# Two-layer diffusion trunk on one core: changes of stage in written order, with twelve modulation chunks

## Chip, cores and metric

One NeuronCore of a Trainium2 chip runs the whole kernel. The metric is the device time of one execution in microseconds; the median of three runs stands for a kernel. TensorE (PE) does matmuls and transposes, ScalarE (ACT) and VectorE (DVE) evict, split and scale, GpSimd (POOL) does only small powers, SyncE (SP) issues nearly all DMA transfers.

## The reference

Two streams of 128 tokens, context (stream 0) and latent (stream 1), go through two layers. Each layer is an attention stage and an MLP stage; each of these normalises the stream, scales and shifts it by a modulation that comes from a conditioning vector, and adds its gated, normalised result to the stream.

```python
for l in range(DEPTH):                       # DEPTH = 2
    m = silu(cvec) @ w_ada[l] + b_ada[l]     # 6 x 2048: shift, scale, gate of both stages
    h = rms_norm(x, g0) * (1 + scale) + shift
    o = mix(h @ w_in[l])                     # neighbourhood, grouped-query, differential heads
    x = x + gate * rms_norm(o @ w_out[l], g1)
    h = rms_norm(x, g2) * (1 + scale') + shift'
    u = square(relu(h @ w_up[l])) @ w_down[l]
    x = x + gate' * rms_norm(u, g3)
```

All is in fp32 accuracy. The weights are some 600 MB, which each execution reads once.

## The kernel before

**Trunk matmuls.** A weight chunk is 1 MB: 128 partitions by 2048 numbers. `split_to` (L1012) cuts each half of it into a high part `wh` (ACT, L1020) and a low part `wl` (DVE, L1021), both rounded to the fast matmul type; three pairs of buffers hold them (`NW = 3`). The activations `XT` (four tiles, one per 512 columns, both streams) are split the same way, and `Group.run` (L350) makes three matmuls per product (L365 to L367) for two streams and two column tiles. A group of eight chunks fills four accumulators in PSUM; the last chunk of a group is run whole, accumulator by accumulator, and each is evicted by `done` when it is full.

**Modulation.** `w_ada` takes two ways. A chunk on PE (`ada_mm`, L139) adds eight narrow matmuls to one PSUM tile; after eight chunks (a set of two blocks) ACT copies it to `pt` (L151), PE transposes that, DVE sums it and makes scale, shift or gate. A chunk on DVE (`dv_mul`, L206) costs two passes over 2048 columns, one per stream, against the rows `sB`. `DV_BLOCKS` and `PE_BLOCKS` at the head of the file say which block goes where.

**Loads.** `items` is the list of chunks in order. `issue` (L1003) asks for the next chunk whenever fewer than `NRAW = 5` raw buffers are in use; all go through SP's queue. Where a PE modulation chunk has been multiplied, or both halves of a weight chunk have been split, its buffer is free. `ahead` (L722) loads four modulation chunks into the XT buffers, which are idle by then.

**A change of stage.** The accumulators of the last group are evicted in the order (tile 2, stream 0), (3, 0), (2, 1), (3, 1). `residual` (L316) sums the squares, raises them to -1/2 on POOL, adds to the stream `x` in four pieces (L326), squares each (ACT, L330) and computes the next norm. `after_attn` (L886) and `after_mlp` (L975) run the chunks left over: four from raw buffers (`TAIL = 4`) and the four held ones. Then `make_xt` (L261) scales a block of 512 columns (DVE for stream 0, L269; ACT for stream 1, L271), transposes it on PE and applies scale and shift (L280, L282), high half (L287) and low half (L288). There are three such changes: layer 0 attention to MLP, layer 0 MLP to layer 1 attention, layer 1 attention to MLP.

**What sets the order.** The program is a list of tiles and operations. A planner orders each engine's instructions: it takes, by a model of times, the first one in written order whose inputs it believes ready; so work written later can get in front. `behind` (L109) forbids this for two pairs: the `wl` splits stay behind the last add of stream 0, and one square of stream 1 stays behind a `pt` copy. `load_sb`, `reload_sb` and `store_x` (L195, L202, L306) are DMA issues that are written behind the handover and are free to be issued earlier.

## Time and profile before

| | us |
|---|---|
| median of 3 runs | 2296.63 (2293.83 to 2298.72) |
| the profiled execution | 2295.36 |
| its span, first to last instruction | 2293.3 |
| PE busy | 2223.2 |
| DVE busy | 1592.6 |
| ACT busy | 1072.2 |

The page of a profile gives busy times, groups of instructions and waits of one execution; the queries on the trace give the same for a stretch. In a timeline a row is: start and length in us, engine, source line, operation, out<-in with shapes, how many instructions were merged, and in brackets the idle time of the engine before it and what ended that. A busy PE may run at half clock, so the granted clock (PEclk, 1.00 is full) has to be read beside it.

### The profile page before, as it was taken

The numbers are of one execution on the slowest core, as the hardware profiler recorded it, in microseconds if no ns is written. First come the engines' busy times: TensorE is split into PE (matmuls) and PEld (weight loads), VectorE is DVE, ScalarE is ACT, GpSimd is POOL, SyncE is SP. The second block draws the span as 40 slices with busy tenths as digits, with TensorE's granted clock in tenths as the row PEclk, the third lists the DMA queues.
The fourth block names the chain that finished last, engine by engine and source line by source line (L and its number), as shares of the span: only waits on it lengthen the run. The fifth ranks groups of instructions, "written<-read, shape, count | busy, mean of one in ns | idle before, by whom it ended". The sixth has DMA issues, their size and how long they took to land.

```text
span 2293.3 us, 26818 instructions
## 1 busy us (share of the span) xinstructions
PE 2223.2 (97%) x10460; PEld 1746.8 (76%) x10460; DVE 1592.6 (69%) x1967; ACT 1072.2 (47%) x1483; POOL 23.3 (1%) x30
## 2 busy tenths in 40 slices
PE   6999999999999999999999999999999999999997
PEld 3667666678888888888867777876888888888886
DVE  2566745499899998999668787548566566565445
ACT  4334444365445434434446455545544543443443
POOL 0000000000000000000000000000000000000000
PEclk9999999999999999999999999999999999999999
DMA  8888787978788887788868666766566566556652
GB/s 335 313 336 333 300 313 309 397 295 298 295 310 300 298 302 294 282 295 313 317 225 299 237 248 218 270 232 230 205 230 233 203 220 236 205 211 223 221 189 93
DMA packets 94539, 611.40 MB, mean 267 GB/s; under 512 B 14026, under 2 KB 16458, under 8 KB 22730
## 3 DMA queue, kind: packets, MB, share of 16 engines
q1 hardware_dynamic: 93836, 609.21, 72.1%
q8 instruction: 82, 1.34, 0.2%
q10 hardware_dynamic: 576, 0.48, 0.1%
q14 instruction: 45, 0.37, 0.0%
HBM read 601.97 MB, written 7.68 MB: 266 GB/s over the span
## 4 chain that ended last, share of the span: by engine, by line
PE 82%; DVE 7%; DMA 4%; ACT 3%; issue 2%; POOL 1%; SPq 0%; POOLq 0%; DVEq 0%; ACTq 0%
PE acc L366 25%; PE acc L367 25%; PE acc L365 25%; DVE wl L1021 3%; PE m L120 3%; PE ada L147 2%; DMA raw<-w_adaT_in 2%; ACT wh L1020 1%; ACT qT L918 1%; DMA raw<-w_in_in 1%; POOL st L107 1%; DMA raw<-w_ada_in 1%; DVE junk L212 1%; PE m L456 1%; DVE stg L326 0%
## 5 line engine op out<-in xcount | busy, mean ns | idle before, releaser
L1020 ACT ACTIVATE wh<-raw 128x1024 fp32r<-128x1024 f32 x720 | 759.2, 1060 | 961.1 <-PE acc L367 862.2
L1021 DVE TENSOR_TENSOR wl<-raw,wh 128x1024 fp32r<-128x1024 f32 x720 | 873.4, 1222 | 471.5 <-ACT wh L1020 469.7
L365 PE MATMUL acc<-wh,XT 128*128 128x512 f32 x1600 | 629.0, 399 | 10.8 <-ACT XT L287 5.9
L366 PE MATMUL acc<-wl,XT 128*128 128x512 f32 x1600 | 629.5, 394 | 4.9 <-DVE wl L1021 4.6
L367 PE MATMUL acc<-wh,XT 128*128 128x512 f32 x1600 | 625.9, 392 | 0.0
L366 PE MATMUL acc<-wl,big 128*128 128x512 f32 x1280 | 500.8, 391 | 1.3 <-DVE wl L1021 1.1
L365 PE MATMUL acc<-wh,big 128*128 128x512 f32 x1280 | 498.3, 393 | 0.6 <-ACT wh L1020 0.3
L367 PE MATMUL acc<-wh,big 128*128 128x512 f32 x1280 | 498.1, 390 | 0.0
L365 PEld LDWEIGHTS acc<-wh,XT 128*128 128x128 f32 x1600 | 301.3, 189 | 91.1 <-ACT wh L1020 14.1
L366 PEld LDWEIGHTS acc<-wl,XT 128*128 128x128 f32 x1600 | 301.9, 189 | 74.0 <-DVE wl L1021 13.4
L367 PEld LDWEIGHTS acc<-wh,XT 128*128 128x128 f32 x1600 | 301.7, 189 | 61.9
L365 PEld LDWEIGHTS acc<-wh,big 128*128 128x128 f32 x1280 | 239.9, 188 | 59.7 <-issue 5.0
L366 PEld LDWEIGHTS acc<-wl,big 128*128 128x128 f32 x1280 | 240.4, 188 | 53.3 <-DVE wl L1021 4.5
L367 PEld LDWEIGHTS acc<-wh,big 128*128 128x128 f32 x1280 | 240.4, 188 | 49.7
L212 DVE SCALAR_TENSOR_TENSOR junk<-raw,sB 128x2048 fp8e5<-128x2048 f32 x92 | 210.4, 2286 | 13.5 <-DMA raw<-w_adaT_in 13.0
L212 DVE SCALAR_TENSOR_TENSOR raw<-raw,sB 128x2048 f32<-128x2048 f32 x92 | 210.1, 2284 | 0.1
L147 PE MATMUL ada<-raw,sT 128*32 128x512 f32 (+1 forms) x768 | 95.0, 574 | 15.2 <-DMA raw<-w_ada_in 15.1
L147 PEld LDWEIGHTS ada<-raw,sT 128*32 128x32 f32 x768 | 20.8, 110 | 60.1 <-issue 36.6
L911 DVE TENSOR_TENSOR big<-tmp,big 128x512 fp32r<-128x512 f32 x64 | 43.8, 687 | 30.1 <-ACT big L910 29.8
L775 DVE TENSOR_TENSOR stg<-stg,acc 128x512 f32<-128x512 f32 x64 | 42.8, 684 | 27.6 <-PE acc L367 27.4
L918 ACT ACTIVATE qT<-acc 128x512 f32<-128x512 f32 x64 | 37.9, 594 | 18.9 <-PE acc L367 17.9
L107 POOL TENSOR_TENSOR st<-st,hf 128x1 f32<-128x1 f32 (+2 forms) x26 | 23.1, 894 | 2263.7 <-DVE st L106 2068.9
(123 smaller groups left out, 919.2 us busy)
## 6 DMA issues: line engine op xcount, KB each, us to landing
raw<-w_up_in SPq DMA_DIRECT2D x128, 1024.0 KB, 5.3
raw<-w_down_in SPq DMA_DIRECT2D x128, 1024.0 KB, 4.9
raw<-w_adaT_in SPq DMA_DIRECT2D x92, 1024.0 KB, 4.9
raw<-w_ada_in SPq DMA_DIRECT2D x80, 1024.0 KB, 7.3
raw<-w_in_in SPq DMA_DIRECT2D x72, 1024.0 KB, 6.4
raw<-w_out_in SPq DMA_DIRECT2D x32, 1024.0 KB, 6.2
XT<-w_ada_in SPq DMA_DIRECT2D x12, 1024.0 KB, 7.8
raw<-w_ada_in SPq DMA_DIRECT2D x16, 512.0 KB, 5.0
```

Source lines behind the costliest of these rows:

```text
L107: pool.tensor_tensor(out, out, hf[:, 0:width], ALU.pow)
L120: pe.transpose(out, in_, ident)
L147: pe.matmul(pa[32 * g:32 * g + 32, 0:w], sT[:, 4 * kq + g, 2 - 2 * t:34 - 2 * t], raw[:, g * w:(g + 1) * w], start=((t, kq) == (0, 0)), st ...
L212: p = dve.scalar_tensor_tensor(o, raw, 1.0, sB[v], ALU.mult, ALU.mult, accum_out=a[:, j, v:v + 1], saturate=None if v else False)
L365: pe.matmul(a, xh, wh[:, c], start=first, stop=False)
L366: pe.matmul(a, xh, wl[:, c], start=False, stop=False)
L367: pe.matmul(a, xl, wh[:, c], start=False, stop=last)
L775: dve.tensor_tensor(o, o, a, ALU.add)
L911: dve.tensor_tensor(A[:, :, 1, s * P:(s + 1) * P], uv, hi.bitcast(F32), ALU.subtract)
L918: act.activation(t, a, AF.Relu)
L1020: act.activation(wh, r, AF.Copy)
L1021: behind(dve.tensor_tensor(wl, r, wh.bitcast(F32), ALU.subtract), mark["res"])
```

## The change

Each change of stage becomes one item, `edge`, with its instructions on PE, ACT, DVE and POOL in the order in which the program is written. From the last chunk of a stage on, every instruction of these four engines is pinned behind the one written before it on its engine (`keep`, `Engine`), until `edge_run` ends; DMA issues on SP are not pinned. `behind` is used there no more.

- Twelve modulation chunks stand at each change: four held in XT buffers, eight from raw buffers (`TAIL = 8`), with the first weight chunk of the new stage loaded behind the fourth. In both attention stages the additional ones come out of the same stage's filling; in the layer 0 MLP one more block of layer 1 (`M_M[3]`, four chunks) goes from DVE to PE. A set that begins at the change has a PSUM tile of its own; the copies to `pt` (`ada_end`) come after the first weight chunk's matmuls.
- `residual` is cut into `res_scale`, `res_add` and `res_norm`; `edge_done` puts these between the evictions and writes a product with the gates after the scale it would delay.
- The first weight chunk is not split ahead: its two halves, and the high part of the third half chunk (the second weight chunk's first half), are split at written places (`split_part`).
- `make_xt` is cut into `xt_turn` (scale, transpose) and `xt_fin` (modulate, split). Block 0 is made in halves, stream 1's first half is turned before stream 0's second half is finished, and the first chunk's matmuls stand between. Block 1 follows; blocks 2 and 3 are made around the next chunks.
- At the end of the kernel the last residual uses the same pieces in the written order.

The core of the diff:

```diff
 NACC = 4
-TAIL = 4
...
-DV_BLOCKS = [G_M, M_A + M_M[:4] + G_A[:3] + G_M]
-PE_BLOCKS = [M_A[2:] + G_A + M_M, M_M[4:] + G_A[3:]]
+DV_BLOCKS = [G_M, M_A + M_M[:3] + G_A[:3] + G_M]
+PE_BLOCKS = [M_A[2:] + G_A + M_M, M_M[3:] + G_A[3:]]
...
+        def __getattr__(self, name):
+            f = getattr(self.e, name)
+            def g(*a, **k):
+                i = f(*a, **k)
+                if mark["keep"]:
+                    tc.keep_in_program_order(i)
+                return i
+            return g
+    pe, act, dve, pool = Engine(nc.tensor), Engine(nc.scalar), Engine(nc.vector), Engine(nc.gpsimd)
+    def keep(on):
+        mark["keep"] = on
...
-        end = t == len(blks) - 1 and kq == 3
+        key = (l, half, *blks)
+        if key not in ada_live:
+            two = mark["keep"] and len(blks) == 2
+            ada_live[key] = [psm() if two else ps.tile([P, 512], F32, tag="ada", bufs=1, name="ada"), 0]
+        pa, no = ada_live[key]
+        ada_live[key][1] += 1
+        end = no == 4 * len(blks) - 1
         for g in range(4):
...
         if end:
+            ada_over.append((l, blks, ada_live.pop(key)[0], 0 if half is None else 2 * half, w))
...
+    ada_over = []
+    def ada_end():
+        while ada_over:
+            l, blks, pa, j0, w = ada_over.pop(0)
             pt = sb([P, 512], "pt")
-            mark["pt"] = act.activation(pt[:, 0:w], pa[:, 0:w], AF.Copy)
-            fast.append(ada_post(l, blks, pt, 0 if half is None else 2 * half, w // P))
+            act.activation(pt[:, 0:w], pa[:, 0:w], AF.Copy)
+            fast.append(ada_post(l, blks, pt, j0, w // P))
 
...
+    def res_scale(ss, s):
         r = st2()
         dve.tensor_reduce(r[:, 0:1], ss[:, s, :], AX.X, ALU.add)
         rstd(r[:, 0:1], r[:, 0:1], D, 1)
+        return r
...
+    def res_add(rows, r, s, last):
         ss2 = st2()
...
+            dve.scalar_tensor_tensor(x[s][:, c], rows[s][:, c], r[:, 0:1], x[s][:, c], ALU.mult, ALU.add)
             if last:
...
+                act.activation(rows[s][:, c], x[s][:, c], AF.Square, accum_out=ss2[:, n:n + 1])
+        return ss2
+    def res_norm(s, ss2):
+        xr[s] = st2()
+        dve.tensor_reduce(xr[s][:, s:s + 1], ss2[:, 0:4], AX.X, ALU.add)
+        rstd(xr[s][:, s:s + 1], xr[s][:, s:s + 1], D, 1)
...
+    def edge_done(rows, ss, s, n, last, mul):
+        if (n, s) == (2, 0):
+            edge["mul"] = mul
+        elif (n, s) == (3, 0):
+            edge["mul"]()
+            edge["r0"] = res_scale(ss, 0)
+            mul()
+        elif (n, s) == (2, 1):
+            edge["ss2"] = res_add(rows, edge["r0"], 0, last)
+            edge["mul"] = mul
+        elif (n, s) == (3, 1):
+            edge["mul"]()
+            if not last:
+                nt[0] = sb([P, 4, 512], "big", 5)
+                res_norm(0, edge["ss2"])
+            edge["r1"] = res_scale(ss, 1)
+            mul()
+            edge["rows"] = rows
+        else:
+            mul()
+    def edge_run(l, w, held, g, ada, part, weights):
+        held(0, 1)
+        for i in range(4):
+            ada(i)
+        held(1, 3)
+        ada(4)
+        new_xt([0])
+        m = xt_turn(0, 0, 0, 2)
+        ada(5)
+        part(0, True, True)
+        part(1, True, False)
+        xt_fin(l, w, 0, 0, m, 0, 2)
+        g.open()
+        g.piece(0, 0, weights(0))
+        m = xt_turn(0, 0, 2, 4)
+        ss2 = res_add(edge["rows"], edge["r1"], 1, False)
+        part(1, False, True)
+        part(2, True, False)
+        res_norm(1, ss2)
+        held(3, 4)
+        ada(6)
+        m1 = xt_turn(0, 1, 0, 2)
+        xt_fin(l, w, 0, 0, m, 2, 4)
+        g.piece(0, 1, weights(1))
+        xt_fin(l, w, 0, 1, m1, 0, 2)
+        part(2, False, True)
+        ada(7)
+        m1 = xt_turn(0, 1, 2, 4)
+        g.piece(1, 0, weights(0))
+        xt_fin(l, w, 0, 1, m1, 2, 4)
+        new_xt([1, 2, 3])
+        m = xt_turn(1, 0, 0, 4)
+        g.piece(1, 1, weights(1))
+        g.cnt += 2
+        xt_fin(l, w, 1, 0, m, 0, 4)
+        ada_end()
+        keep(False)
+        xt_fin(l, w, 1, 1, xt_turn(1, 1, 0, 4), 0, 4)
+    def edge_items(l, w, tail, held, first):
+        items.append(("edge", tail[:4] + [first] + tail[4:], (l, w, held)))
...
+                mul = lambda: dve.tensor_tensor(S["rows"][s][:, c], S["rows"][s][:, c], a, ALU.mult)
+                edge_done(S["rows"], ssA[0], s, nt, False, mul)
...
-                if (nt, s) == (3, 0):
-                    residual(S["rows"], ssA[0], False, 0)
...
+            go = Group(2, KT, o_lhs(), wout_done(nh))
+            go.final = nh == 1
+            rest += tchunks(I["w_out"][l], 8 * nh, 8, go, ko, need)
...
-        weave(rest[cut:], fill[nf:], tail=TAIL)
...
-        def after_attn(S=S, l=l, use=use):
-            mark["tail"] = mark["pt"]
-            use()
-            drain_dv()
-            drain_fast()
-            new_xt()
-            mark["pt"] = mark["tail"]
-            residual(S["rows"], ssA[0], False, 1)
-        call(after_attn)
...
-            last = ada_items(1, G_A[3:] + M_M[4:5])
-            load, use = ahead(last[4:])
+            last = ada_items(1, M_M[4:5] + M_M[3:4] + G_A[3:])
+            load, use = ahead(last[8:])
...
+        first = rest.pop(0)
+        edge_items(l, 1, *end_attn, first)
+        rest.insert(0, ("call", lambda l=l: (drain_fast(), make_xt(l, 1, 2))))
+        rest.insert(2, ("call", lambda l=l: (drain_fast(), make_xt(l, 1, 3))))
...
-            g, m = dv_items(0, G_M), dv_items(1, M_A + M_M[:4])
+            g, m = dv_items(0, G_M), dv_items(1, M_A + M_M[:3])
...
-        def after_mlp(M=M, l=l, use=use):
-            if l + 1 < L:
-                mark["tail"] = mark["pt"]
-                use()
-                mark["pt"] = mark["tail"]
-            drain_fast()
-            residual(M["rows"], ssA[1], l == L - 1, 1)
...
+    def split_part(k, hi, lo):
+        i, j = subs[k]
+        if i not in raws:
+            return False
+        r = raws[i][:, j * 1024:(j + 1) * 1024]
+        if hi:
             wh = wp.tile([P, 1024], F32R, tag="wh", bufs=NW, name="wh")
             wl = wp.tile([P, 1024], F32R, tag="wl", bufs=NW, name="wl")
             act.activation(wh, r, AF.Copy)
-            behind(dve.tensor_tensor(wl, r, wh.bitcast(F32), ALU.subtract), mark["res"])
             splits[(i, j)] = (wh, wl)
+        if lo:
+            wh, wl = splits[(i, j)]
+            dve.tensor_tensor(wl, r, wh.bitcast(F32), ALU.subtract)
             state["split"] += 1
             if j == 1:
                 del raws[i]
                 state["live"] -= 1
                 issue()
+        return True
...
+        if it[0] == "edge":
+            l, w, held = it[2]
+            at = [i for i, c in enumerate(it[1]) if c[0] == "t"][0]
+            no = [i for i in range(len(it[1])) if i != at]
+            g, ksub = it[1][at][2:4]
+            k0 = sub_no[(ci + at, 0)]
+            def ada(i, ci=ci, lst=it[1]):
+                ada_mm(*lst[no[i]][2], raws.pop(ci + no[i]))
+                state["live"] -= 1
+                issue()
+            def weights(j, ci=ci):
+                wh, wl = splits[(ci + at, j)]
+                return [(ksub[j][0], wh, wl)]
+            edge_run(l, w, held, g, ada, lambda k, hi, lo: split_part(k0 + k, hi, lo), weights)
+            ci += len(it[1])
+            continue
         if it[0] == "ada":
             r = raws.pop(ci)
...
+            if whole and g.final:
+                split_to(k0 + 1)
+                keep(True)
             for j in range(2):
-                split_to(sub_no[(ci, j)] + NW - 1)
+                if not (whole and g.final):
+                    split_to(k0 + j + NW - 1)
...
+                    if g.final:
+                        break
...
```

`xt_turn` holds the first lines of `make_xt` (L261: L269 or L271 and the transposes), `xt_fin` its rest; `Group.piece` is the inner loop of `Group.run` for one stream.

## Rows read from the trace of the kernel before

**Rows 1.** The page's head and its first part: engine, busy us and share.
```profile
span 2293.3 us, 26818 instructions
...
PE 2223.2 (97%) x10460; PEld 1746.8 (76%) x10460; DVE 1592.6 (69%) x1967; ACT 1072.2 (47%) x1483; POOL 23.3 (1%) x30
```

**Rows 2.** Windows of 4 us: length, busy us by engine, PEclk, DMA share, GB/s.
```profile
core 0: us, PE busy (x) PEld busy (x) DVE busy (x) ACT busy (x) POOL busy (x), PEclk, DMA share, GB/s
...
456.00:460.00 4.00, 2.97 (x28) 1.10 (x28) 3.06 (x14) 1.96 (x6) 1.11 (x2) 1.00 0.97 375
...
1204.00:1208.00 4.00, 2.08 (x8) 1.64 (x9) 3.49 (x10) 2.81 (x6) 0.72 (x1) 0.50 1.01 426
...
1560.00:1564.00 4.00, 2.88 (x9) 2.46 (x10) 2.15 (x6) 2.75 (x8) 0.32 (x1) 0.50 0.65 274
1564.00:1568.00 4.00, 4.00 (x19) 3.33 (x18) 2.43 (x7) 1.99 (x6) 0.00 (x0) 0.80 0.00 2
```

**Rows 3.** Timeline of TensorE at the first change.
```profile
452.70 1.92 PE L147 MATMUL ada<-raw,sT 128*32 128x512 f32 x16
457.03 0.66 PE L120 MATMUL m<-cs,pt 128*128 128x128 f32 x4 [2.40 <-ACT pt L151]
...
460.81 1.07 PE L147 MATMUL ada<-raw,sT 128*32 128x512 f32 x8 [0.41 <-DMA raw<-w_ada_in]
...
466.48 0.66 PE L120 MATMUL m<-cs,pt 128*128 128x128 f32 x4 [1.17 <-ACT pt L151]
...
469.23 0.50 PE L365 MATMUL acc<-wh,XT 128*128 128x512 f32 x1 [1.22 <-ACT XT L287]
```

**Rows 4.** Timeline of TensorE at the second change.
```profile
1199.43 0.66 PE L120 MATMUL m<-cs,pt 128*128 128x128 f32 x4 [1.14 <-ACT pt L151]
1200.63 0.63 PE L120 MATMUL m<-cs,big 128*128 128x128 f32 x4 [0.54 <-DVE big L269]
1205.92 0.79 PE L365 MATMUL acc<-wh,XT 128*128 128x512 f32 x1 [4.66 <-ACT XT L287]
...
1210.35 0.51 PE L365 MATMUL acc<-wh,XT 128*128 128x512 f32 x1
```

**Rows 5.** Timeline of TensorE at the third change.
```profile
1547.38 3.64 PE L147 MATMUL ada<-raw,sT 128*32 128x512 f32 x32
1550.83 3.62 PE L147 MATMUL ada<-XT,sT 128*32 128x512 f32 x32
1557.01 0.66 PE L120 MATMUL m<-cs,pt 128*128 128x128 f32 x4 [2.56 <-ACT pt L151]
...
1561.12 1.11 PE L120 MATMUL m<-cs,big 128*128 128x128 f32 x4 [3.02 <-ACT big L271]
```

**Rows 6.** Timeline of TensorE at the end: the step from matmul to matmul.
```profile
2280.66 0.39 PE L366 MATMUL acc<-wl,big 128*128 128x512 f32 x1
2280.89 0.39 PE L367 MATMUL acc<-wh,big 128*128 128x512 f32 x1
```

**Rows 7.** The page's costliest groups: busy us, mean ns of one, idle before.
```profile
L1020 ACT ACTIVATE wh<-raw 128x1024 fp32r<-128x1024 f32 x720 | 759.2, 1060 | 961.1 <-PE acc L367 862.2
L1021 DVE TENSOR_TENSOR wl<-raw,wh 128x1024 fp32r<-128x1024 f32 x720 | 873.4, 1222 | 471.5 <-ACT wh L1020 469.7
...
L212 DVE SCALAR_TENSOR_TENSOR junk<-raw,sB 128x2048 fp8e5<-128x2048 f32 x92 | 210.4, 2286 | 13.5 <-DMA raw<-w_adaT_in 13.0
```

**Rows 8.** TensorE's waits, 500 to 1186 (layer 0 MLP): total us, times, longest.
```profile
PE acc L366 <- DVE wl L1021: 1.3, 2, 0.8
```

**Rows 9.** One load of 1 MB, issued at 1163.76: issue to landing.
```profile
DMA to landing us min/median/max: 4.9/4.9/4.9
```

**Rows 10.** Timeline of VectorE at the end: four adds of a residual.
```profile
2287.36 2.74 DVE L326 SCALAR_TENSOR_TENSOR stg<-stg,st 128x512 f32<-128x512 f32 x4 [0.66 <-POOL st L107]
```

**Rows 11.** Timeline of SP at the second change.
```profile
1191.29 0.33 SPq L204 DMA_DIRECT2D sB<-silu  x1
...
1198.77 0.33 SPq L204 DMA_DIRECT2D sB<-silu  x1
1199.14 0.70 SPq L309 DMA_DIRECT2D xd<-stg  x1
```

More of the change, by code (lines that the diff above doesn't have):

```diff
@@ L314, in load_x @@
             nc.sync.dma_start(x[s], xd[s])
-    def residual(rows, ss, last, s):
-        if not last and s == 0:
-            nt[0] = sb([P, 4, 512], "big", 5)
+    def res_scale(ss, s):
         r = st2()
@@ L983, in trunk @@
-        call(after_mlp)
+            items.extend(rest[103:])
+            call(lambda M=M: (res_add(M["rows"], edge["r1"], 1, True), keep(False)))
     def drain_dv():
@@ L991, in drain_fast @@
             step_list(fast, 1)
-    chunks = [it for it in items if it[0] != "call"]
+    chunks = [c for it in items if it[0] != "call" for c in (it[1] if it[0] == "edge" else [it])]
     raws = {}
@@ L1027, in split_to @@
                 issue()
+        return True
+    def split_to(k):
+        while state["split"] <= min(k, len(subs) - 1):
+            if not split_part(state["split"], True, True):
+                return
     ci = 0
```

183 lines of the change are left out of this document (92 added, 91 removed).

## Prediction

> **What bounds the kernel now.** I call the three points where one stage hands over to the next the changes: the first (layer 0, attention to MLP), the second (layer 0 MLP to layer 1 attention), the third (layer 1, attention to MLP). T is the end of the last matmul of the old stage; times after T are written +x.
>
> The page comes first: TensorE is busy 97% of a span of 2293.3 us [rows 1], so only what keeps it idle or slow can be won. The windows of 4 us show where that is: around the changes it works part of the time while the DMA engines are full (share 1.01, 426 GB/s), and behind the second and third its granted clock stands at 0.50, the lower level of 1.2 GHz [rows 2]. The timeline of TensorE gives the holes:
>
> - First change, T = 452.6: idle 2.40, 0.41, 1.17 and 1.22, in sum 5.2 us; the clock stays at 1.00 [rows 2, 3].
> - Second, T = 1191.2: idle 1.14, 0.54 and 4.66, in sum 6.3. The matmul that ends the last hole runs at the lower clock, until 1210.35: 4.43 us of work at half speed, 2.2 lost. Together 8.5 [rows 2, 4].
> - Third, T = 1547.3: idle 2.56 and 3.02, in sum 5.6, then again some 4.4 us at the lower clock, 2.2 lost. Together 7.8 [rows 2, 5].
>
> So 21.5 us is all that a perfect handover could give back. The releasers in the brackets say what the holes are: the copy of the modulation sums (pt) with transposes queued behind it, the scaled rows (big), and XT.
>
> **The change, part by part.** TensorE's stock at a change grows to twelve modulation chunks: four held in XT buffers before T, eight through the raw buffers. A chunk is 0.86 us (four between 1547.38 and 1550.83) [rows 5]. At the first change ten already stand behind T before (the pair at 452.70, four ahead of the XT ones, four in XT), at the others eight. At the first and third the additional ones come from earlier in the same stage, so TensorE's work is unchanged. At the second, four come from VectorE's queue in the layer 0 MLP: 4 x 0.86 = 3.45, and their set needs four pt transposes more, about 0.5: **+3.95**. On VectorE this saves eight passes of 2.29 us [rows 7], but in that MLP TensorE waits for VectorE's splits only 1.3 us in all [rows 8]: **-1.0**, bounds -1.6 and 0.
>
> The copies of pt move behind the whole handover, so the holes that begin with them go (2.40, 1.17, 1.14, 2.56). What is late next? I walk the written order from T, with durations of before: a chunk 0.86, a matmul every 0.23 [rows 6], a half-chunk split 1.06 on ScalarE and 1.22 on VectorE [rows 7], four residual adds 2.74 [rows 10], a 1 MB load 4.9 from its issue when alone [rows 9], and, when loads queue, at 426 GB/s 2.46 behind the one ahead of it [rows 2].
>
> Only five raw buffers exist. At T they hold chunks 0 to 3 of the eight and the first weight chunk. Chunk 4 can be asked for only when chunk 0 has been multiplied: a held chunk and chunk 0 end at +1.7, so it lands at +6.7. Chunks 5, 6, 7 follow at +9.2, +11.6, +14.1, and the second weight chunk, whose buffer is chunk 4's, at **+16.5**.
> TensorE has done three held chunks and chunks 0 to 3 at +6.0 and waits 0.7 for chunk 4; two transposes; it waits 1.3 for chunk 5 (+9.2 to +10.1); six matmuls with the first half chunk; two transposes; the last held chunk and chunk 6, to +13.4. Next in its order are stream 1's first transposes. They need ScalarE to scale stream 1, and ahead of that on ScalarE stands the early split of the third half chunk, which waits for +16.5 and ends at +17.6. Queued behind it on ScalarE are that scaling, the high halves of stream 0's second half and of stream 1. The transposes start at +18.1: idle **4.6**. Then six matmuls, chunk 7, two transposes, six matmuls; the turn of stream 0's next block stands on VectorE behind the low half of stream 1 and costs 1.1. Idle in sum 0.7 + 1.3 + 4.6 + 1.1 = **7.7** a change.
>
> Had the transfers been there, the chain alone would decide: low half of stream 0 at about +9, four adds 2.74, a split 1.22, then sum, power on GpSimd (VectorE waited 0.66 for one [rows 10]) and scaling, transposes at about +14.9. Idle 0.7 + 2.8 + 1.1 = 4.6 a change. That is the lower bound. The upper one is 7.7 plus a clock loss of 2.2: the hole of 4.6 us is as long as the 4.66 at the second change, whose end saw the lower clock [rows 2, 4], while holes up to 2.4 with chunks around them left it at 1.00 [rows 2, 3]. I take half, 1.1.
>
> A page rates the transfers otherwise: the Trainium skill, "DMA: Bandwidth & Descriptors" (Where 436 GB/s comes from), holds that loads from HBM are bound near 358 GB/s a core. This trace moves 426 [rows 2]; by the page's figure a load would take 2.9 and my estimate of the sum would be some 7 us more. The trace decides.
>
> The second change has further transfers. Before, the reload of sB was issued as soon as its last reader had finished (1191.29 and 1198.77) and the store of x[0] right behind (1199.14), although both are written later [rows 11]. Neither is pinned by the change, so they again get ahead: sB's first half lands before chunk 4 and costs nothing, the store and the second half (1 MB each) push chunks 5 to 7 and the second weight chunk back by 2 x 2.46. Idle 7.7 + 4.9 = 12.6, and the hole before stream 1's transposes, 7.1, is past any doubt on the clock: 2.2.
>
> Small edits: the early scale factor of stream 0 and the deferred products are hidden by seven chunks (0 to +6.0) at every change; uncovered they would be worth half a microsecond. Blocks 2 and 3 of XT are made during the next three weight chunks, 16 us of matmuls, in which ScalarE has room; uncovered, up to 3 us each. Dropping the order marks on wl and on the squares costs nothing once the order is written. At the very end the last residual begins a little earlier, since the scale of stream 0 no longer waits for a product: **-0.3**, bounds -0.7 and +0.3.
>
> On ScalarE's parked split the trace of before has no example of landed work standing behind a load. The Trainium skill, "PSUM — Partial Sum Buffer" (Engine vs sequencer instructions), says that ScalarE's, VectorE's and GpSimd's queues are strict FIFO. By that the 4.6 stands; an engine that let ready work pass would start the transposes near +15.6 and save about 2 us a change.
>
> **The sum.** First change: 7.7 + 1.1 - 5.2 = +3.6. Second: 12.6 + 2.2 + 3.95 - 8.5 = +10.2. Third: 7.7 + 1.1 - 7.8 = +1.0. MLP -1.0, end -0.3. In all +13.5 us. The profiled run took 2295.36 (2.1 around its span), so it would become 2308.9; the runs' median of 2296.63 lies 1.3 above it, which gives **2310**.
>
> **The rivals.**
> 1. *The chain rules, not the transfers* (ends faster). If the loads are there in time (the buffers are asked for earlier than I read, or weights pass the chunks), idle is 4.6 a change and the clock holds: 4.6 - 5.2 = -0.6; 4.6 + 3.95 - 8.5 = 0; 4.6 - 7.8 = -3.2; with -1.3 in sum -5.1, so **2291.5**. It decides from the point at which the second weight chunk lands before about +13. For it: the holes removed are real, and DMA is idle late in the third change (0.65 [rows 2]). Against: five loads of 2.46 cannot fit between +1.7 and +13 with a first latency of 4.9.
> 2. *The written waits stand, the intruders don't* (store and reload stay behind the weights, clock at 1.00 everywhere). +2.5, 7.7 + 3.95 - 8.5 = +3.2, -0.1, -1.3: +4.3, **2301**. For it: order of issue may differ. Against: rows 11.
> 3. *The change doesn't do what it says*: other ready work gets between the pinned instructions and fills the holes, or holes just move. Within 2 us of before, **2297**. Little speaks for it, as all work behind the handover needs the second weight chunk.
> 4. *Worse than forecast*: the loads at the first change start late, since its stage already runs the queues full, or XT's later blocks come too late; 5 us more, **2315**.
>
> **How the numbers follow.** Forecast 0.44, rival 1 0.18, rival 2 0.20, rival 3 0.08, rival 4 0.10. A measurement of this kernel tells apart about 0.2%, 4.6 us. Faster by more: most of rival 1, 0.16. Within: the rest of 1, half of 2, most of 3 (0.02 + 0.10 + 0.06): 0.19 with a hair of the forecast. Slower: 0.65. The range must reach from rival 1 to beyond rival 4: 2291 to 2318. The forecast's own range, by its bounds, is 2303 to 2316.
>
> **What would show it.** In the changed kernel's timeline: TensorE waits for w_ada loads near +6 and +8, ScalarE sits before a wh for the second weight chunk, TensorE sits until about +18 at the first and third change and until about +23 at the second, and the granted clock is 0.50 behind the second. No wait for pt is left. If the second weight chunk lands before +13, or the wh stands behind stream 1's scaling, the step fails and the time moves towards rival 1. The layer 0 MLP should be shorter by 1 us at most.

## The result and the profile after

The changed kernel takes 2313.37 us (median), 1.007 times the kernel before, interval 1.0053 to 1.0087; measured again among the experiments it took 2313.20, ratio 1.0075 (1.0056 to 1.0095). It is 16 to 17 us slower. One of the first four executions took 5429.16 us and has no part in the ratio; the other three have a median of 2311.95. The profiled execution took 2311.95, with a span of 2310.1.

All instructions that go through the new wrapper carry one line, L82, so after the change one goes by tiles. First the head of the page after, beside [rows 1]:

```profile
span 2310.1 us, 26881 instructions
...
PE 2237.1 (97%) x10496; PEld 1749.0 (76%) x10496; DVE 1577.5 (68%) x1955; ACT 1074.5 (47%) x1487; POOL 25.5 (1%) x30
```

TensorE is busy 13.9 us longer, with 36 instructions more (four chunks of eight and four transposes); part of the rest is matmuls at half clock, which count as busy. Where the time went is seen by stretches. Each kernel is cut at the three T, 40 us behind each T, and behind the first once more 50 us later; columns as in [rows 2], idle time is the length minus PE's busy time. Windows of the kernel before:

```profile
452.60:492.60 40.00, 34.80 (x211) 23.36 (x211) 34.83 (x73) 29.84 (x60) 2.00 (x4) 1.00 0.75 290
492.60:542.60 50.00, 50.00 (x229) 41.04 (x228) 49.51 (x50) 24.20 (x30) 0.00 (x0) 1.00 0.87 315
542.60:1191.20 648.60, 646.18 (x2885) 529.25 (x2883) 562.22 (x571) 295.87 (x336) 0.00 (x0) 1.00 0.80 293
1191.20:1231.20 40.00, 33.66 (x189) 23.65 (x189) 34.72 (x70) 28.50 (x61) 2.69 (x4) 0.91 0.80 297
1231.20:1547.30 316.10, 309.48 (x1457) 248.82 (x1455) 220.56 (x311) 152.71 (x251) 7.74 (x6) 0.99 0.69 250
1547.30:1587.30 40.00, 34.42 (x192) 24.35 (x192) 34.18 (x65) 28.37 (x59) 1.66 (x3) 0.91 0.52 197
```

and of the changed kernel:

```profile
450.04:490.04 40.00, 34.38 (x203) 19.94 (x203) 26.02 (x61) 25.45 (x53) 1.66 (x3) 0.91 0.79 307
490.04:540.04 50.00, 43.00 (x184) 34.55 (x183) 40.30 (x46) 23.48 (x33) 0.00 (x0) 0.90 0.68 239
540.04:1204.94 664.90, 662.19 (x2955) 542.33 (x2954) 564.07 (x567) 301.25 (x340) 0.64 (x1) 1.00 0.78 287
1204.94:1244.94 40.00, 34.41 (x200) 20.03 (x200) 28.11 (x57) 26.28 (x58) 1.96 (x4) 0.91 0.87 334
1244.94:1557.52 312.58, 308.60 (x1446) 250.40 (x1444) 227.46 (x324) 154.92 (x255) 9.65 (x6) 1.00 0.68 248
1557.52:1597.52 40.00, 32.96 (x196) 18.68 (x196) 24.67 (x58) 24.41 (x53) 1.64 (x3) 0.91 0.69 266
```

The second row of each carries most of it: behind the first change the kernel before is busy for all 50 us at full clock, the changed one stands idle for 7.0 us and shows a clock of 0.90. A PEclk of 0.91 over 40 us is some 7 us at the lower level, about 3 us of work lost; behind the first change this is new (1.00 before).

| stretch | before | after | difference | of it chunks moved or added |
|---|---|---|---|---|
| start to first T | 452.6 | 450.0 | -2.6 | -1.7 |
| first to second T | 738.6 | 754.9 | +16.3 | +1.7 |
| second to third T | 356.1 | 352.6 | -3.5 | +0.5 |
| third T to last matmul | 734.0 | 740.7 | +6.8 | +3.45 |
| behind the last matmul | 12.0 | 11.8 | -0.2 | 0 |
| span | 2293.3 | 2310.1 | +16.8 | +3.95 |

The changes themselves look as the prediction walked them. TensorE of the changed kernel at the first change (answers to [rows 3]), then the hole before stream 1's transposes at the second and third ([rows 4, 5]):

```profile
457.34 1.07 PE L82 MATMUL m<-raw,sT 128*32 128x512 f32 x8 [1.08 <-DMA raw<-w_ada_in]
459.78 1.94 PE L82 MATMUL m<-raw,sT 128*32 128x512 f32 x8 [1.01 <-DMA raw<-w_ada_in]
...
469.45 0.52 PE L82 MATMUL m<-cs,big 128*128 128x128 f32 x2 [3.53 <-ACT big L82]
...
1224.47 0.69 PE L82 MATMUL m<-cs,big 128*128 128x128 f32 x2 [2.50 <-ACT big L82]
...
1577.14 0.69 PE L82 MATMUL m<-cs,big 128*128 128x128 f32 x2 [5.28 <-ACT big L82]
```

ScalarE and GpSimd at the first change say why:

```profile
467.95 1.06 ACT L82 ACTIVATE wh<-raw 128x1024 fp32r<-128x1024 f32 x1 [3.77 <-DMA raw<-w_up_in]
468.91 0.49 ACT L82 ACTIVATE big<-stg,st 128x256 f32<-128x256 f32 x1
```

```profile
464.95 0.55 POOL L82 TENSOR_TENSOR st<-st,hf 128x1 f32<-128x1 f32 x1 [10.55 <-DVE st L82]
```

The scale of stream 1 (`st`) was there at 465.5. The scaling (`big<-stg,st`) starts at 468.91, since the early split ahead of it on ScalarE had waited 3.77 us for the second weight chunk. At the second and third change the same wait is 4.24 and 4.36.

What the prediction had not walked is a stall 70 us behind the first T, where the first evictions of the MLP fall. TensorE, ScalarE (the last of its evictions and what stands behind) and VectorE there:

```profile
523.85 1.30 PE L82 MATMUL acc<-wh,XT 128*128 128x512 f32 x3 [2.59 <-ACT wh L82]
529.31 0.80 PE L82 MATMUL acc<-wl,XT 128*128 128x512 f32 x1 [4.16 <-DVE wl L82]
```

```profile
521.61 0.58 ACT L82 ACTIVATE tmp<-m 128x512 f32<-128x512 f32 x1
522.22 0.63 ACT L82 ACTIVATE big<-tmp 128x512 fp32r<-128x512 f32 x1
522.75 2.93 ACT L82 ACTIVATE wh<-raw 128x1024 fp32r<-128x1024 f32 x3
```

```profile
523.49 2.28 DVE L82 SCALAR_TENSOR_TENSOR junk<-raw,sB 128x2048 fp8e5<-128x2048 f32 x1
...
525.82 2.29 DVE L82 SCALAR_TENSOR_TENSOR raw<-raw,sB 128x2048 f32<-128x2048 f32 x1
...
528.03 3.49 DVE L82 TENSOR_TENSOR wl<-raw,wh 128x1024 fp32r<-128x1024 f32 x3
```

The planner put four evictions ahead of three `wh` and two modulation passes ahead of three `wl`. The weights were not late: the load issued at 503.15 landed at 514.00 and the next at 516.45, both before TensorE stood still. With matmuls at the lower clock until about 535 (some 3.0 us lost, an estimate from the granted clock) the stall costs 7.0 + 3.0 = 10 us. Nearby on SP's queue stand transfers that the kernel before issued at 520 to 560, the constants of layer 1:

```profile
487.58 0.42 SPq L775 DMA_DIRECT2D bcs<-qg_in  x1
...
499.41 0.85 SPq L792 DMA_DIRECT2D rpbz<-cv  x1
...
503.15 2.92 SPq L1111 DMA_DIRECT2D raw<-w_up_in  x1
```

### The profile page after: what moved, and what is told of

It reads as the page before. It is cut to its first block, busy times and chain, and to the rows that moved or that the text cites. A ratio compares the mean times of both kernels' runs of the same rounds, so it can differ in the third digit from the quotient of the medians.

```text
span 2310.1 us, 26881 instructions
## 1 busy us (share of the span) xinstructions
PE 2237.1 (97%) x10496; PEld 1749.0 (76%) x10496; DVE 1577.5 (68%) x1955; ACT 1074.5 (47%) x1487; POOL 25.5 (1%) x30
## 4 chain that ended last, share of the span: by engine, by line
PE 84%; DVE 5%; DMA 5%; ACT 3%; issue 2%; POOL 0%; POOLq 0%; DVEq 0%; ACTq 0%
PE acc L82 77%; PE m L82 5%; PE ada L82 3%; DVE wl L82 2%; DMA raw<-w_adaT_in 2%; DMA raw<-w_ada_in 1%; ACT wh L82 1%; DVE junk L82 1%; DMA raw<-w_in_in 1%; DMA raw<-w_up_in 1%; DVE stg L82 1%; ACT qT L82 1%; DVE raw L82 1%; POOL st L82 0%; ACT tmp L82 0%
## 5 line engine op out<-in xcount | busy, mean ns | idle before, releaser
L82 ACT ACTIVATE wh<-raw 128x1024 fp32r<-128x1024 f32 x720 | 759.2, 1060 | 972.8 <-PE acc L82 846.4
L82 DVE TENSOR_TENSOR wl<-raw,wh 128x1024 fp32r<-128x1024 f32 x720 | 874.9, 1223 | 474.6 <-ACT wh L82 467.2
L82 PE MATMUL acc<-wh,XT 128*128 128x512 f32 x3200 | 1028.5, 397 | 7.6 <-ACT wh L82 7.5
L82 PE MATMUL acc<-wh,big 128*128 128x512 f32 x2560 | 800.6, 391 | 0.0
L82 PEld LDWEIGHTS acc<-wh,XT 128*128 128x128 f32 x3200 | 604.5, 189 | 151.7 <-ACT wh L82 17.0
L82 PE MATMUL acc<-wl,XT 128*128 128x512 f32 x1600 | 632.0, 395 | 7.4 <-DVE wl L82 7.0
L82 PEld LDWEIGHTS acc<-wh,big 128*128 128x128 f32 x2560 | 480.4, 188 | 107.5 <-issue 4.0
L82 PE MATMUL acc<-wl,big 128*128 128x512 f32 x1280 | 500.6, 391 | 1.8 <-DVE wl L82 1.7
L82 PEld LDWEIGHTS acc<-wl,XT 128*128 128x128 f32 x1600 | 303.2, 189 | 77.3 <-DVE wl L82 16.3
L82 PEld LDWEIGHTS acc<-wl,big 128*128 128x128 f32 x1280 | 240.4, 188 | 52.9 <-DVE wl L82 4.8
L82 DVE SCALAR_TENSOR_TENSOR junk<-raw,sB 128x2048 fp8e5<-128x2048 f32 x88 | 201.3, 2288 | 19.1 <-DMA raw<-w_adaT_in 18.9
L82 DVE SCALAR_TENSOR_TENSOR raw<-raw,sB 128x2048 f32<-128x2048 f32 x88 | 201.2, 2286 | 0.1
L82 DVE TENSOR_TENSOR stg<-stg,acc 128x512 f32<-128x512 f32 x128 | 85.3, 684 | 46.1 <-PE acc L82 38.0
L82 PE MATMUL ada<-raw,sT 128*32 128x512 f32 (+1 forms) x704 | 89.1, 572 | 15.3 <-DMA raw<-w_ada_in 14.4
L82 DVE TENSOR_TENSOR big<-tmp,big 128x512 fp32r<-128x512 f32 x64 | 43.7, 689 | 34.8 <-ACT big L82 34.8
L82 PEld LDWEIGHTS ada<-raw,sT 128*32 128x32 f32 x704 | 19.8, 110 | 58.2 <-issue 34.1
L82 DVE TENSOR_REDUCE st<-m 128x2 f32<-128x512 f32 (+3 forms) x45 | 23.1, 529 | 49.7 <-PE m L82 49.5
L82 PEld LDWEIGHTS m<-cs,big 128*128 128x128 f32 x224 | 26.3, 143 | 32.7 <-ACT big L82 16.3
L82 POOL TENSOR_TENSOR st<-st,hf 128x1 f32<-128x1 f32 (+2 forms) x26 | 25.3, 976 | 2278.3 <-DVE st L82 2195.6
L82 PE MATMUL m<-cs,big 128*128 128x128 f32 x224 | 36.8, 284 | 12.7 <-ACT big L82 11.3
L82 ACT ACTIVATE qT<-acc 128x512 f32<-128x512 f32 x64 | 38.0, 594 | 21.3 <-PE acc L82 20.1
L82 ACT ACTIVATE stg<-acc 128x512 f32<-128x512 f32 x52 | 30.7, 596 | 35.7 <-PE acc L82 35.3
```

What stands on the lines that cost most here:

```text
L82: i = f(*a, **k)
```

## Experiments

Theory: the early split that parks ScalarE makes the largest hole of each change, and an order of the planner's makes the stall. Two things limit how the runs can be read: an edit can shift the planner's order far away, and of all kernels here only the changed one has the stall. So runs are compared by stretches, and 10 of the first 20 us gained are the stall's wherever it went.

**The early split moved (undoes one part).**

```diff
         part(1, False, True)
-        part(2, True, False)
         res_norm(1, ss2)
...
-        part(2, False, True)
+        part(2, True, True)
         ada(7)
```

> The early wh of the third half chunk (ScalarE) is moved behind the turn of stream 1, next to its wl; nothing else. Theory A, the parked split: in the changed kernel ScalarE begins that wh only when the second weight chunk has landed (about +18 at each change) while the scale of stream 1 was ready on GpSimd at about +15.5, so the scaling queued behind it loses 3.4, 3.9 and 4.0 us and TensorE idles 3.53, 2.50 and 5.28 us before the transposes of stream 1. With the split out of the way these holes shrink to under 1.5 us each: 8 to 10 us less idle, and where no hole over 2.5 us is left the stretch at the lower clock behind the change (2.6 to 3.2 us lost at each) goes too. In sum -9 to -18 us, about 2300. Rival B, the chain or the loads of the modulation chunks hold the transposes anyway: the holes only move by under 1 us, time within 2 us of the changed kernel (2313).

Measured: 2290.88 us, 0.997 of the kernel before (0.996 to 0.9979): faster than both. The transposes of stream 1 now follow with no wait at the first two changes. TensorE at the first change, where only the waits for chunks 4 and 5 (3.25 and 0.73) are left, and at the third:

```profile
460.04 1.09 PE L82 MATMUL m<-raw,sT 128*32 128x512 f32 x8 [3.25 <-DMA raw<-w_ada_in]
...
469.54 0.44 PE L82 MATMUL m<-cs,big 128*128 128x128 f32 x2
...
1558.17 0.44 PE L82 MATMUL m<-cs,big 128*128 128x128 f32 x2 [1.61 <-ACT big L82]
```

By stretches against the changed kernel: first to second T -13.0 (10 of it the stall), second to third -2.5, third to the end -5.4. So by the stretches the parked split cost 11 us, within what theory A gave (9 to 18); the other 10 are a shift of the planner's order that the theory had not foreseen. The medians put it somewhat lower: from the run with the constants held below, which has the split early and no stall, to this one they fall by 8.4. The lower clock went at the third change alone; at the first two it still costs 3.05 and 3.2. Rival B is out. The Trainium skill, "PSUM — Partial Sum Buffer" (Engine vs sequencer instructions), says that ScalarE's queue is strict FIFO; the scaling that was ready at 465.5 and started at 468.91 agrees.

**The second weight chunk asked for earlier.** The order of loads alone:

```diff
+    order = list(range(len(chunks)))
...
+            order[no + 7:e + 1] = [e] + list(range(no + 7, e))
...
-            i = state["dma"]
+            i = order[state["dma"]]
```

> Only the order in which loads are asked for is changed: the second weight chunk of the new stage ahead of modulation chunks 6 and 7 (two places earlier in the queue, about 5 us). Theory A, the parked split waits for this load: the wh starts at about +13, no longer last, the scaling of stream 1 starts when its scale is ready (+15.5), and TensorE now waits instead for chunk 6 (landing near +16): transposes about +17 instead of +19.5, 2 to 3 us a change, plus part of the clock loss: -6 to -14 us. Rival B, the transfers don't matter (the chain rules): within 2 us of 2313. Rival C, the modulation chunks were the binding loads: chunks 6 and 7 come 2.5 us later each and the time grows by 3 to 8 us.

Measured: 2292.95, ratio 0.9987 (0.9977 to 0.9996). Without the stall's 10 us it gains 10 on the changed kernel, inside theory A's 6 to 14. The hole before the transposes is gone at all three changes; instead TensorE waits 2.38 us for chunk 6 at the third, as expected. The same effect, then, from the other end: it is the load that ScalarE was parked for.

**Layer 1's constants held at their written place.**

```diff
+    def late_dma(*a):
+        behind(nc.sync.dma_start(*a), mark["up"])
...
-            nc.sync.dma_start(bcs[:, i, :], I[nm][l:l + 1, :].to_broadcast([P, P]))
+            late_dma(bcs[:, i, :], I[nm][l:l + 1, :].to_broadcast([P, P]))
```

(the same for the other loads of `layer_consts` and for `load_cache`; `mark["up"]` is the latest square of `up_evict`.)

> The loads of layer 1's constants (head-norm gains, lambda, relative-position rows, the first cache load) are held at the place where they are written, late in the layer 0 MLP; in the changed kernel the planner issued them at 487 to 499 us, among the first weight chunks of that MLP. Theory A: those transfers, and the order that the planner made around them (four up-evictions ahead of three wh, two modulation passes ahead of three wl), are the cause of the stall of TensorE at 521 to 529 (2.59 and 4.16 us) and of the lower clock behind it: the stall goes, -8 to -11 us, about 2303. Rival B: the stall comes from the MLP's own start (weights late behind the change, splits in arrears) and stays or turns up some us later: within 2 us of 2313.

Measured: 2299.30, ratio 1.0018 (1.0006 to 1.003), 14 us under the changed kernel, 3 more than theory A's most. Of the 50 us from 490.92 on TensorE is busy 49.93 at full clock. ScalarE at the same evictions:

```profile
519.61 0.63 ACT L82 ACTIVATE big<-tmp 128x512 fp32r<-128x512 f32 x1
520.14 1.04 ACT L82 ACTIVATE wh<-raw 128x1024 fp32r<-128x1024 f32 x1
521.09 0.58 ACT L82 ACTIVATE qT<-acc 128x512 f32<-128x512 f32 x1
```

The splits are back between the evictions. The parked split stays: the hole before the transposes is 5.27 at the third change. Theory A holds for "the loads of the constants and the order around them"; the next but one run separates the two.

**The order left free.** No instruction is pinned:

```diff
                 i = f(*a, **k)
-                if mark["keep"]:
-                    tc.keep_in_program_order(i)
                 return i
```

> The same code in the same written order, but no instruction at the changes is pinned to it: the planner may reorder. Theory A, the pinned order is what parks ScalarE: the free order lets the scaling of stream 1 pass the split, holes before its transposes go, -6 to -15 us. Rival B, the planner's order is the written one in all that matters: within 3 us of 2313. Rival C, the free order lets pt copies, modulation passes and other splits back in between: slower by 5 us or more, or at best the 2296 of the kernel before, with TensorE's waits on pt and on splits back in the timeline.

Measured: 2297.57, ratio 1.0001 (0.9991 to 1.001). The stall is absent; second to third T is 1.5 us shorter than in the changed kernel, third to the end 6.0 (no wait over 1.1 us there). At the first change the planner's own order still leaves TensorE 4.10 us before transposes. So without the pins the rewritten changes are worth nothing against the kernel before, as rival C's mild form has it, and pinned they are worth what the pinned order is worth: -5 us with the split late, +17 with it early, of which 10 are the stall outside the pinned stretch.

**The constants early, with the splits in good order** (on top of the late split):

```diff
-            rest.insert(1, ("call", load_sb))
+            rest.insert(1, ("call", lambda l=l: (load_sb(), layer_consts(l + 1))))
...
-            call(lambda l=l: layer_consts(l + 1))
```

> On top of the late split: the loads of layer 1's constants are written, and so issued, among the first weight chunks of the layer 0 MLP, as the planner had put them in the changed kernel; here the planner's order on ScalarE and VectorE keeps the wh and wl between the up-evictions. Theory A, the order on the engines made the stall at 521 to 529, not the transfers: no stall near 520, time within 2 us of the late split (2291). Rival B, the transfers themselves (many small packets; a 1 MB load beside them took 10.85 us) held the weights up: a stall of 3 us or more returns between 490 and 530, 2294 to 2301.

Measured: 2292.94, ratio 0.9987 (0.9975 to 0.9999); against the late split, by the two ratios, +0.0017 with about 0.0015 either way. The largest hole there:

```profile
505.68 0.50 PE L82 MATMUL acc<-wl,XT 128*128 128x512 f32 x1 [1.47 <-DVE wl L82]
```

It is a wait for VectorE, which works without a pause there and has a modulation pass and the sum of the constants' bias rows ahead of three `wl`:

```profile
501.59 2.29 DVE L82 SCALAR_TENSOR_TENSOR raw<-raw,sB 128x2048 f32<-128x2048 f32 x1
...
503.80 0.68 DVE L82 TENSOR_TENSOR biasB<-biasB,cs 128x512 f32<-128x512 f32 x1
504.41 3.49 DVE L82 TENSOR_TENSOR wl<-raw,wh 128x1024 fp32r<-128x1024 f32 x3
```

The stall of 2.59 and 4.16 does not return. The constants were issued earlier here than in the changed kernel (the store to `rpbz` at 477.96 against 499.41), so the run does not repeat its transfers exactly; but there both loads had landed, at 514.00 and 516.45, before TensorE stood still at 521.26. It was the order on ScalarE and VectorE. Why the planner chose it in that one kernel is not shown.

**The changed kernel again.**

> The changed kernel itself, a second look beside the others. Theory A, the stall at 521 to 529 is in its order and comes every time, as do the holes of 2.5 to 5.3 us before the transposes of stream 1: 2311 to 2315 again, those holes within 0.5 us of the first look; the waits for chunk 4 and the stretches at the lower clock may differ by some us, since kernels with the same order at the first change waited 0 to 3.25 us there. Rival B, they are chance of one execution: holes elsewhere.

Measured: 2313.20. TensorE at the stall and before the transposes:

```profile
522.95 0.96 PE L82 MATMUL acc<-wh,XT 128*128 128x512 f32 x3 [2.59 <-ACT wh L82]
528.41 0.79 PE L82 MATMUL acc<-wl,XT 128*128 128x512 f32 x1 [4.50 <-DVE wl L82]
```

```profile
470.07 0.44 PE L82 MATMUL m<-cs,big 128*128 128x128 f32 x2 [1.56 <-ACT big L82]
...
1222.06 0.69 PE L82 MATMUL m<-cs,big 128*128 128x128 f32 x2 [3.40 <-ACT big L82]
...
1577.85 0.69 PE L82 MATMUL m<-cs,big 128*128 128x128 f32 x2 [5.29 <-ACT big L82]
```

The stall is in the order and comes again. The holes before the transposes are not stable to 0.5 us as expected: 1.56 here, 3.53 in the execution shown above. TensorE came later to that place: it had waited 2.07 instead of 1.08 for chunk 4, and its clock had been at the lower level for 6.8 us instead of 3.4 (460.1 to 467.0 here). The sum of idle time of a change is steadier (4.9, 5.6, 6.9 against 5.6, 5.6, 7.0), so single holes must not be compared.

**What is next late, once the split is out of the way.** Three single edits on the late split:

```diff
-        held(0, 1)
         for i in range(4):
             ada(i)
-        held(1, 3)
+        held(0, 3)
```

> On top of the late split: the four modulation chunks of the raw buffers are multiplied before the first held one, so that their buffers come free, and chunks 4 to 7 and the second weight chunk are asked for, 0.86 us earlier at each change. Theory A, the loads still set the pace (with the late split TensorE waited 3.25, 2.13 and 0.62 us for chunk 4): each of these holes is shorter by up to 0.86, 2 us in all, and where the hole before the lower clock falls below about 1.5 us (second change) the 3 us lost there go as well: 2286 to 2289. Rival B, the queue is full in any case at the first change and the chain of stream 0 is next at the others: within 1 us of 2291.

Measured: 2291.83, ratio 0.9981 (0.9968 to 0.9994): no gain that can be told. The waits for chunk 4 did shrink by 0.9 and 0.6 at the first two changes, but at the second, a wait of 1.50 for chunk 5 and one of 1.13 for stream 1's scaling took their place, and a stretch at the lower clock that was gone there (0 instead of 3.2) was met by one of 3.4 in the attention, at 1419 to 1426.

```diff
-            nc.sync.dma_start(sB[v], sB_d[v:v + 1, :].to_broadcast([P, D]))
+            behind(nc.sync.dma_start(sB[v], sB_d[v:v + 1, :].to_broadcast([P, D])), mark["xt"])
```

> On top of the late split: the reload of sB is held behind the second change; with the late split its first half was issued 0.2 us before the end of the old stage's matmuls, ahead of chunk 4. Theory A, the intruder costs its 2.46 us of transfer: the wait for chunk 4 (2.13 us) goes, and with no hole over 1 us left at the second change the 3.2 us at the lower clock go too: 2286 to 2289. Rival B, the other chunks' loads or the chain take its place: hole only moved, within 1 us of 2291. Rival C, the modulation passes of layer 1 that read sB start later and TensorE waits for them in the attention: slower by 2 us or more.

Measured: 2292.05, ratio 0.9983 (0.9972 to 0.9995): rival B. TensorE at the second change waits less for chunk 4 and more for chunk 5:

```profile
1200.00 1.07 PE L82 MATMUL m<-raw,sT 128*32 128x512 f32 x8 [0.59 <-DMA raw<-w_ada_in]
...
1203.75 1.06 PE L82 MATMUL m<-raw,sT 128*32 128x512 f32 x8 [2.32 <-DMA raw<-w_ada_in]
```

(2.13 and 0.45 with the reload ahead.) What one load gives up, the next one waits for.

```diff
-        m1 = xt_turn(0, 1, 0, 2)
         xt_fin(l, w, 0, 0, m, 2, 4)
         g.piece(0, 1, weights(1))
+        m1 = xt_turn(0, 1, 0, 2)
         xt_fin(l, w, 0, 1, m1, 0, 2)
```

> On top of the late split: stream 1 is turned behind stream 0's second half (its low half and its six matmuls) instead of ahead of it. The order on VectorE and SyncE is the same; on TensorE the two transposes move behind six matmuls, on ScalarE the scaling of stream 1 moves behind the high half of stream 0's second half. Theory A, this part is a small gain: the chain of stream 1 starts about 0.4 us later and its matmuls have 1.4 us less cover: 0.5 to 1.5 us more idle a change, +2 to +4 us. Rival B, the place doesn't matter since the loads rule: within 1 us of 2291. Rival C, the six matmuls fill the hole before the transposes: up to 1.5 us a change shorter, -2 to -4 us.

Measured: 2294.13, ratio 0.9994 (0.9981 to 1.0006), 0.0024 above the late split: theory A. New holes of 1.30 stand behind chunk 7, before stream 1's matmuls, at the first two changes. Turning stream 1 ahead is worth about 3 us by the medians (2294.13 against 2290.88); the difference of the ratios has about 0.0015 either way.

**How many chunks.** Eight at the second change alone on the late split, then, with one edit more, eight everywhere:

```diff
...
-PE_BLOCKS = [M_A[2:] + G_A + M_M, M_M[3:] + G_A[3:]]
+PE_BLOCKS = [M_A[2:] + G_A + M_M, M_M[4:] + G_A[3:]]
...
-            last = ada_items(1, M_M[4:5] + M_M[3:4] + G_A[3:])
-            load, use = ahead(last[8:])
+            last = ada_items(1, G_A[3:] + M_M[4:5])
+            load, use = ahead(last[4:])
...
```

> On top of the late split: at the second change only, eight modulation chunks instead of twelve; the four others go back to VectorE's queue in the layer 0 MLP, as in the kernel before. Theory A, added work on TensorE costs what it takes and the holes there are set by loads and chain: 4 x 0.86 us and the transposes of their sums leave TensorE (-3.95), two waits for chunks 4 and 5 go too, the second weight chunk lands 10 us earlier, but 3.4 us of cover is missing: the stretch from the second to the third change gets 2 to 5 us shorter and the layer 0 MLP up to 1 us longer, about 2288. Rival B, the chunks only fill time that TensorE would otherwise idle: holes grow by the 3.9 us that the work shrinks, 2290 to 2292. Rival C, longer holes bring more of the lower clock: slower, 2293 or more.

Measured: 2288.08, ratio 0.9957 (0.9941 to 0.9974), the fastest here. Second to third T is 346.3 against 350.1 with the late split alone: -3.8, the four chunks and their transposes. Idle time and clock there are level: 5.0 + 1.7 lost instead of 3.0 + 3.2. The layer 0 MLP did not get longer. The rest of the profile's gain (7.2 in all) is 3 us at the lower clock that this execution did not have at the first change, where the order is the same; so the gain over the late split is about 4 us by this one profile, which the two ratios alone (-0.0013, about 0.0019 either way) don't settle.

```diff
-TAIL = 8
+TAIL = 4
```

> On top of the late split: eight modulation chunks at all three changes. At the first and third the four chunks that leave are multiplied earlier in the same stage, so TensorE's work falls only at the second (by 3.95, as in the run with eight there alone: profiled span 2282.5). Theory A, chunks that belong to the stage anyway are free cover: without them 3.4 us of cover is missing at the first and third change while only 0.6 to 1.0 us waits for chunks 4 and 5 go: idle grows 1 to 3 us a change over the run with eight at the second, 2290 to 2294. Rival B, loads set the end of the holes: five fewer loads ahead of the second weight chunk make up for the cover, within 1.5 us of the run with eight at the second (2288).

Measured: 2301.79, ratio 1.0025 (1.0011 to 1.0038), 14 us above eight at the second change alone and more than either theory gave. The changes at first and third are each 2 us worse (4.9 + 1.7 and 5.2 + 1.5 of idle and lost time against 4.1 + 0 and 4.3 + 0). The larger part, 7.6 us beside the 3.45 that the moved chunks themselves take, lies ahead of the first T, where the four chunks now stand among the weights of the output projection and TensorE idles 3.27 us, ScalarE waiting for a load:

```profile
410.60 2.00 ACT L82 ACTIVATE wh<-raw 128x1024 fp32r<-128x1024 f32 x2 [2.88 <-DMA raw<-w_out_in]
```

A modulation chunk is 1 MB of transfer for 0.86 us of TensorE, so in a stretch that is short of transfers it costs more than its matmuls.

**A version ahead of both kernels**: late split, eight chunks at the second change, constants held (the edits above together).

> The late split, eight chunks at the second change, and the layer 1 constants held at their written place: a version meant to stand ahead of both kernels. Theory A, the three gains are independent, and the last has nothing left to give where no stall is: 2286 to 2289, under the kernel before by 0.3 to 0.45%. Rival B, the planner's order shifts with each edit and a new stall turns up: 2290 or more, with a hole of over 2 us away from the changes.

Measured: 2289.41, ratio 0.9966 (0.9953 to 0.9978). That is just above theory A's 2286 to 2289, and the new hole of rival B is not there (none over 2 us away from the changes). No different from eight at the second change alone (0.9957): holding the constants has nothing left to give once the stall is gone. Nor do the ratios of these two and of the late split alone (0.9970) tell the three kernels apart. By the stretch from the second to the third T eight chunks are better: the five profiles with the split late and twelve chunks there take 348.9 to 352.2 us for it, this one takes 348.2 and the one above 346.3, about 3 less on the average. The version to keep is the late split with eight chunks at the second change, by that stretch; that the whole kernel gains by the eight chunks is not shown.

## Why the prediction was right and where it was not

The total was right: 2310 forecast, 2313.4 measured, in the range and in the forecast's own. Its distribution was not, and the agreement is in good part luck: a stall of 10 us that nothing in the forecast stands for took the place of some 6 us of intruders and lower clock at the second change that did not come, and 4.3 us were won in a stage that it left out. Idle time plus work lost at the lower clock, from the windows above:

| step | predicted | measured |
|---|---|---|
| first change | 7.7 + 1.1 - 5.2 = +3.6 | 5.6 + 3.2 - 5.2 = +3.6 |
| second change, added work | +3.95 | -3.8 when taken away again |
| second change, idle and clock | 12.6 + 2.2 - 8.5 = +6.3 | 5.6 + 3.2 - 8.7 = +0.1 |
| third change | +1.0 | 7.0 + 2.6 - 7.8 = +1.8 |
| layer 0 MLP | -1.0 | +10 (stall), +0.3 (the rest) |
| layer 1 attention | 0 | -4.3 |
| ahead of the first T | 0 | -0.9 |
| end | -0.3 | -0.2 |
| in no row | | +2.4 |

**Right: the parked split.** Walked: the second weight chunk lands at +16.5, ScalarE's split ends at +17.6, the transposes start at +18.1. Measured: the split starts at +17.9 to +18.1 and the transposes at +19.4 to +19.6. No wait for pt is left at the changes, as forecast. That the split holds the transposes is shown by moving it and by moving its load. The +15.6 that the prediction gives for a scaling that is not held up stands there without its working; with the late split the transposes start at +15.6 at the third change, but at +19.0 at the first, behind the wait of 3.25 for chunk 4. Idle time is then 4.4, 3.0 and 4.0 a change, so the 4.6 of the chain alone was no lower bound. The idle time was set too high (7.7 against 5.6 and 7.0) and the clock loss too low (1.1 against 3.2 and 2.6): taking half of 2.2 was the wrong choice, and the upper bound of 2.2 was no bound. That both sums at the first change are +3.6 is luck.

**Wrong: the intruders at the second change.** The step said that store and reload get ahead of chunks 5 to 7. Only the first half of sB's reload did (issued at 1204.78, just before T); the second came at 1229.09 and the store of x at 1240.97. In [rows 11] they went early because their last readers had finished; here the planner let the loads of the new stage go first. That was rival 2's condition, with the lower clock added. The step took a place in a planned queue from one plan and carried it into another.

**Wrong: the layer 0 MLP.** "Dropping the order marks costs nothing once the order is written" and the -1.0 for fewer modulation passes looked only at the pinned stretch. The rest of the stage was planned anew, and 10 us went there (9 in the second look: 7.3 idle, 1.7 lost). No row of before could show this; what the prediction lacked was a term for it, since a change that rewrites the order of one stretch leaves a planner free to reorder the next.

**Not foreseen: the layer 1 attention** is 4.3 us better (idle 4.0 instead of 6.6, clock 1.00 instead of 0.99); in the second look it has the same idle time and 1.7 us at the lower clock again, so only the 2.6 of idle time come every time. One of the kernel before's holes there, 1.35 us some 165 us behind the second T, comes back as 1.38 at that distance in the run with eight chunks everywhere, so four chunks fewer in that stage are the likely cause; no run tests it alone.

**The sum by rivals.** Rival 1 (the chain rules, 2291.5) did not happen, but the late split comes out at its number by removing what kept the chain from ruling. In part that is luck: 4.3 us of its gain are the attention's, and its first change still loses 3.05 to the lower clock, which rival 1 had at nothing. Rival 4's cause for the first change, loads that start late, was seen in single executions (3.25 us for chunk 4 with the late split, 1.04 with eight at the second, the same order there).

## What to carry to other kernels

When an order is written out by hand, look in it for each instruction that waits for a transfer and ask what stands behind it on its engine: an early split that nobody needs yet cost 8 to 11 us because ready work queued behind it. Cover made of work that needs its own loads pays only where transfers are not what runs short, and work that is moved from an engine with room to the bound one costs it most of its time (here about 3 us of 3.95). And after pinning one stretch, read the stretches that were not pinned: the largest single loss lay 70 us behind the change.

## What the runs showed of the hardware

**The clock fell after holes of one microsecond.** The prediction took holes up to 2.4 us as harmless, from [rows 2, 3]. In the changed kernel the granted clock at the first change fell to its lower level (0.50, 1.2 GHz) behind holes of 1.08 and 1.01; windows of 4 us there:

```profile
452.00:456.00 4.00, 4.00 (x40) 1.04 (x32) 2.09 (x9) 2.43 (x8) 1.11 (x2) 1.00 0.89 342
456.00:460.00 4.00, 1.91 (x18) 0.56 (x18) 1.95 (x3) 1.27 (x2) 0.00 (x0) 0.93 1.01 426
460.00:464.00 4.00, 4.00 (x16) 1.76 (x8) 3.92 (x7) 2.59 (x9) 0.00 (x0) 0.64 1.01 420
464.00:468.00 4.00, 1.93 (x17) 0.42 (x16) 1.41 (x5) 0.23 (x3) 0.55 (x1) 1.00 1.02 428
```

Of the pinned kernels with nearly the same order there, the seven with a wait of 1.66 to 3.25 us in that place all went to the lower level, of four with waits of 0.72 to 1.28 one did, the changed kernel; these falls cost 1.5 to 3.2 us each. The stretch at the lower level in the layer 1 attention (3.4 us lost at 1419 to 1426 in one run, 1.7 in the kernel before) also comes in some executions only. So a difference of 3 us between two profiles can be the clock alone.

**Transfers ran at 428 GB/s on this one core** in the window above. The Trainium skill, "DMA: Bandwidth & Descriptors" (Where 436 GB/s comes from), holds that loads from HBM are bound near 358; this trace doesn't show that bound, and the walk at 2.46 us a load stands.

**Small transfers delay large ones beyond their bytes.** Beside the constants' transfers, one 1 MB load of the changed kernel, issued at 503.15, took 10.8 us from issue to landing, against 4.9 alone [rows 9]. Part of that is another 1 MB load ahead of it, issued at 502.01 and landed at 511.55. But from 506 to 508, beside the small packets of the store to `rpbz`, the DMA engines are as full as from 512 to 514 (share 1.01 in both) and move 219 GB/s instead of 426:

```profile
raw<-w_up_in SPq DMA_DIRECT2D x1, 1024.0 KB, 10.8
```
